# Low halves of ten FFN weight blocks by an accumulating DMA in a fused fp32 transformer step on one Trainium2 core

## The chip, the cores and the metric

The kernel runs on one core of a Trainium2 chip. The metric is the device time of one execution in microseconds (us); lower is better. Three executions of the kernel before took 1033.17, 1029.07 and 1034.92 us, median 1033.17.

## The reference, cut to what matters

One step of a small diffusion backbone: a mixing block (attention, S5 and RG-LRU scans) and then a convolutional gated FFN, over 640 tokens (128 context and 512 latent), all in fp32. The change touches the FFN only:

```python
def conv_ffn(h, lp):
    a, b = jnp.split(h @ lp['ffn_w_up'], 2, axis=-1)      # 640 x 1024 times 1024 x 5632
    a = dw_conv(a, lp['ffn_conv_w'], lp['ffn_conv_b'], 1, 1)
    return (jax.nn.gelu(a) * b) @ lp['ffn_w_down']        # 640 x 2816 times 2816 x 1024

h = rms_norm(x, lp['g2']) * (1 + sc2) + sh2
x = x + gt2 * conv_ffn(h, lp)
```

## The kernel before, in words

**Split products.** Every fp32 product is made of three TensorE products. A block is split into a high part, its rounding to the matmul type (`sh` for weights), and a low part, the block minus the high part (`sl`). The three products are high by high, high by low and low by high. `split` (L115) makes the two parts of a 128x512 weight block: the high part by an activation copy on ScalarE (ACT, helper line L79), the low part by a subtraction on VectorE (DVE, helper line L82). Both have six buffers.

**The FFN's up projection.** FF is 2816 = 22 tiles of 128 columns, numbered `fi`. For one tile the weights of both halves (a and b) are four 128x512 quarters `a11`, `a12`, `a21`, `a22` of two raw tiles `wr` (for the tiles 2 and 3 these are four tiles `wq`). Instead of eight quarter products the kernel makes seven, M1 to M7, in Winograd's way: sums of quarters (`sums_a`, `sums_b`, on VectorE and GpSimd) against sums of the four quadrants of the normalised tokens (`x_terms`). Each product M is 12 matmuls of 320 columns (`prod_mm`: for each of four k-slices high by high, high by low, low by high, in this order). M1, M2 and M3 use the quadrants as they are (`xbh`, `xbl`), M6, M7 and M5 use sums (`xth`, `xtl`).

**The stage of the change.** Between the output projection of the mixer and the steady run over the FFN tiles stands a hand-ordered head (L1619 to L1662), in which DVE, ACT and PE follow the program's order; POOL (GpSimd) does so in the whole kernel. The head takes the first two FFN tiles (fi 0 and 1, `NHEAD` is 2), while the normalisation of the last token tile (t = 4) is still under way. `prepare(n)` splits the next weight blocks, `early` issues their products, `post` adds them up. The order of blocks is M1 and M2 of tile 0, M1 and M2 of tile 1, then M3, M6, M7 of both:

```python
prepare(2)                      # split M1, M2 of tile 0
sums_b(0)                       # overwrites a11 and a12 of tile 0
out_mm(4, bl, 0, w_out2); norm2_t(3, ...); out_mm(4, bl, 1, w_out2)
out_res(4, bl, slice(512, 1024))
norm2(4, ...); prepare(4)       # split M1, M2 of tile 1
early(0, 1); sums_b(1); prepare(6)
norm2_t(4, None); early(2, 3)
early(4, 5); prepare(8); early(6, 7); prepare(10); early(8, 9)
```

The lines that only sum or split tokens are left out here. `sums_b(fi)` adds the sum `s2` to `a11` and subtracts it from `a12` in place; so it has to come after the splits of M1 and M2 have read these quarters, and M3 reads the `a12` that it leaves. `out_res(4)` makes the residual of the last token tile, `norm2(4)` its norm (a square sum on ACT, a power `rs` on POOL, a diagonal `dg` on DVE), and `norm2_t(4)` its transposes on PE and the scaling on ACT and DVE.

**DMAs.** The weights come by DMAs of the SP queue. POOL issues a few DMAs itself: eight accumulating ones `tsp<-tgate` (L541, SBUF to DRAM, 320 KB each) in the mixer and the loads `gt<-gdr` (L1147).

Of the kernel before, what the change touches and what calls it, by code (L numbers as in the profile page):

```python
# [18 lines left out]
MUL, ADD, SUB, MAX = ALU.mult, ALU.add, ALU.subtract, ALU.max  # L19
# [17 lines left out]
NPR = 3  # L37
S4F = 2
KPOW = 1
PREP_1 = 7  # L40
NB = 2
GE = True
# [5 lines left out]
NHEAD, LOOK, SA_AT, SB_AT = 2, 4, "M5", "M2"  # L48
# [23 lines left out]
def tile_hybrid_flow_step(ctx, tc, a, o):  # L72
    nc = tc.nc
    ctx.enter_context(tc.manual_schedule(engines={mybir.EngineType.Pool}))
    V, S, G, T, Q = nc.vector, nc.scalar, nc.gpsimd, nc.tensor, nc.sync
    SE, TE, FE, XE = V, V, V, G

    def act(out, in_, f=AF.Copy, **k):
        S.activation(out, in_, f, **k)  # L79

    def tt(out, x, y, op, e=V):
        e.tensor_tensor(out, x, y, op)  # L82
# [7 lines left out]
    def f(ap):  # L90
        return ap.bitcast(F32)
# [23 lines left out]
    def split(src, p=None, e=V):  # L115

        b, p = (6, pw) if p is None else (4, p)
        n = src.shape[-1]
        hi = p.tile([P, n], F32R, tag="sh", name="sh", bufs=b)
        act(hi, src)  # L120
        lo = p.tile([P, n], F32R, tag="sl", name="sl", bufs=b)
        tt(lo, src, f(hi), SUB, e)
        return hi, lo

    def wload(src, p=None):
        raw = raw_load(src)
        return [split(raw[:, z * 512:z * 512 + 512], p) for z in range(2)]
# [312 lines left out]
    def h_chunk(k, b, m2):  # L440
        b2 = b[:, 256:260]
        for q in range(2):
            mm(b2[:, 2 * q:2 * q + 2], m2[:, q * P:(q + 1) * P], sel[:, 0:2], True, True)
        sc = px.tile([P, 2], F32, tag="sc", name="sc", bufs=2)
        sh = px.tile([P, 2], F32, tag="sh", name="sh", bufs=2)
        ts(sh, b2[:, 0:2], pp("b_ada", k, 1), None, ADD, ALU.bypass)
        ts(sc, b2[:, 2:4], pp("b_ada", 8 + k, 1), 1.0, ADD, ADD)
        ts(sc, sc, pp("g1", k, 1), None, MUL, ALU.bypass)
        hf = px.tile([P, NT], F32, tag="hf", name="hf", bufs=2)
        for q, (n0, n1) in ((0, (NC_, NT)), (1, (0, NC_))):  # L450
            act(hh[:, k, n0:n1], xt[:, k, n0:n1], AF.Identity, scale=sc[:, q:q + 1], bias=sh[:, q:q + 1])
            ts(hf[:, n0:n1], xt[:, k, n0:n1], sc[:, q:q + 1], sh[:, q:q + 1], MUL, ADD)
        tt(hl[:, k], hf, f(hh[:, k]), SUB)
# [19 lines left out]
    for k in range(NK + 1):  # L473
        if k < NK:
            ads.append(ada_mm(k))
        if k < 2:
            h_chunk(k, *ads[k])
            if k == KPOW:
                s5_powers(px)
# [42 lines left out]
    def gate_half(br, c, h, x=None):  # L522

        if h == 0:
            state["wg"] = win(18 + 8 * br + c)
            state["tg"] = pv.tile([P, NT], F32, tag="tgate", name="tgate", bufs=2)
            if br:
                raw = pw.tile([P, 256], F32, tag="wr", name="wr", bufs=4)
                Q.dma_start(out=raw, in_=a["w_br"][c][:, 256 + 256 * br:512 + 256 * br])
                state["wb"] = split(raw)  # L530
        tg = state["tg"]
        n0, n1 = h * HT, (h + 1) * HT
        b = bank()
        dense_half(state["wg"], hh, hl, b[:, :HT], n0, n1)
        act(tg[:, n0:n1], b[:, :HT], AF.Tanh, scale=0.5)
        if br:
            b = bank()
            dense_half([state["wb"]], *x, b[:, :HT], n0, n1, nk=2)
            stt(tg[:, n0:n1], tg[:, n0:n1], 1.0, b[:, :HT], ADD, MUL)
        if h and br == 1:  # L540
            G.dma_start(out=tsp[16 + c], in_=tg, accum_op=ADD)  # L541
        elif h:
            Q.dma_start(out=tsp[8 * br + c], in_=tg)
# [118 lines left out]
    for i in range(2):  # L662
        b = dense_fm(win(12 + i), hh, hl)
        if i == 0:
            for _ in range(PREP_1):
                next(prep)
# [4 lines left out]
        for t0 in range(4):  # L671
            Q.dma_start(out=ut[32 * t0:32 * t0 + 32, 4 * i:4 * i + 4],
                        in_=udr[i].rearrange("(j f) t c -> t f j c", f=32)[t0])
    ylru = []

    def lru_tile(i):
# [9 lines left out]
        lw = pw.tile([P, 4, P], F32, tag="wr", name="lw", bufs=4)  # L686
        Q.dma_start(out=lw, in_=a["lru_w"][i])
        lwh, lwl = (x.rearrange("p (m c) -> p m c", m=4) for x in split(lw.rearrange("p m c -> p (m c)")))
        yield
        hs = []  # L690
# [596 lines left out]
    for qt in range(2):  # L1287
        w = [wload(a["w_out"][qt, kk]) for kk in range(2)]
# [31 lines left out]
    ups, s2s = {}, {}  # L1320
# [9 lines left out]
    def raw_free():  # L1330
        freed[0] += 1
        raw_pump()
# [11 lines left out]
    def quarters(fi):  # L1344
        if fi in AHEAD:
            return rawt["up", fi] + rawt["up", NF + fi]
        r0, r1 = rawt["up", fi], rawt["up", NF + fi]
        return r0[:, 0:512], r0[:, 512:], r1[:, 0:512], r1[:, 512:]

    def sums_a(fi):  # L1350

        a11, a12, a21, a22 = quarters(fi)
        tt(a21, a11, a21, SUB, SE)
        s2s[fi] = p1.tile([P, 512], F32, tag="s2", name="s2", bufs=2)
        tt(s2s[fi], a22, a21, SUB, SE)

    def sums_b(fi):

        a11, a12, a21, a22 = quarters(fi)
        s2 = s2s[fi]  # L1360
        tt(a11, s2, a11, ADD, SE)
        tt(a12, a12, s2, SUB, (V if fi < S4F else G))
# [5 lines left out]
    def prod_prep(fi, m):  # L1368
        a11, a12, a21, a22 = quarters(fi)
        if m == "M6" and fi not in s2s:  # L1370
            sums_a(fi)
        w = split({"M1": a11, "M2": a12, "M3": a12, "M4": a22, "M5": a11, "M6": s2s.get(fi), "M7": a21}[m])
        if fi >= NHEAD and m == SB_AT:
            sums_b(fi)
        if (m in ("M3", "M4") and fi >= NHEAD or m == "M4") and fi not in AHEAD:
            raw_free()
            if fi < NHEAD:
                raw_free()
        if m == SA_AT and NHEAD <= fi + 1 < NF and ("up", NF + fi + 1) in rawt:
            sums_a(fi + 1)  # L1380
        return w
# [123 lines left out]
    def add_up(fi, ms):  # L1505
        for m in ms:
            items.append((lambda fi=fi, m=m: prod_prep(fi, m), lambda w, fi=fi, m=m: prod_run(fi, m, w)))
# [278 lines left out]
```

## Time and profile before

| | before |
|---|---|
| three executions, us | 1033.17, 1029.07, 1034.92 |
| median, us | 1033.17 |
| the profiled execution's own time, us | 1037.32 |
| its span, us | 1035.6 |
| mean granted TensorE clock | 0.986 |
| PE busy | 996.1 us, 96% |
| VectorE (DVE) busy | 771.5 us, 74% |
| ScalarE (ACT) busy | 473.4 us, 46% |
| GpSimd (POOL) busy | 129.3 us, 12% |

The span is the time from the first to the last instruction of one profiled execution. Its own time of 1037.32 us is 4.15 us above the median of the three. The stage of the change lies between about 559 and 640 us of the span. PE's records there are read with care: matmuls are pipelined, so a busy PE need not be one at its peak, and idle time is what a wait shows.

### The profile page before, as it was taken

How to read it: one execution, taken by the hardware profiler on the slowest of the kernel's cores; microseconds unless marked ns; L12 is line 12 of the kernel's file. 1: busy time of each engine (PE TensorE's matmuls, PEld its weight loads, DVE VectorE, ACT ScalarE, POOL GpSimd, SP SyncE). 2: the span in 40 equal slices, each digit the busy share in tenths (PEclk: the TensorE clock that was granted, in tenths of full speed). 3: DMA queues.
4: the chain of work that ended last, by engine and by line, in shares of the span. 5: the costliest groups of instructions: out<-in, count | busy, mean ns of one | idle time of the engine just before them, and what ended most of it. 6: DMA issues, size and time to landing. Idle time of an engine off the chain costs nothing.

```text
span 1035.6 us, 17667 instructions
## 1 busy us (share of the span) xinstructions
PE 996.1 (96%) x6636; PEld 925.0 (89%) x6636; DVE 771.5 (74%) x1820; ACT 473.4 (46%) x919; POOL 129.3 (12%) x147
## 2 busy tenths in 40 slices
PE   5998999999999999999999989999999999999996
PEld 4788986879999999999899988988999899988995
DVE  6893787565846766657566599976998589966986
ACT  5253772224355555555332755532554145522543
POOL 6017500000002021101000201100110001100113
PEclk9998999999999999999999999999999999999998
DMA  9523357673245235434844131141324122331212
GB/s 363 217 82 88 97 169 247 228 238 115 77 131 170 76 100 136 117 81 115 291 142 142 51 129 47 41 143 34 92 82 123 58 69 79 99 102 48 95 63 102
DMA packets 50582, 126.31 MB, mean 122 GB/s; under 512 B 5536, under 2 KB 17728, under 8 KB 50496
## 3 DMA queue, kind: packets, MB, share of 16 engines
q1 hardware_dynamic: 48768, 120.46, 36.0%
q0 software_dynamic: 1728, 4.72, 2.2%
q8 instruction: 52, 0.85, 0.3%
q14 instruction: 34, 0.28, 0.1%
HBM read 111.10 MB, written 12.75 MB: 120 GB/s over the span
## 4 chain that ended last, share of the span: by engine, by line
PE 76%; DVE 10%; DMA 6%; ACT 3%; issue 2%; POOL 1%; SPq 1%; POOLq 0%; DVEq 0%; ACTq 0%
PE bk L94 34%; PE bM L94 23%; PE dn L94 14%; DMA wr<-in_w_in 3%; DVE sl L82 2%; DMA kc<-in_kct 1%; PE ptp L1066 1%; PE sc L94 1%; PE ob L94 1%; DMA xin<-in_x_sample 1%; PE gp L94 1%; ACT h L79 1%; DVE x L82 1%; ACT sh L79 1%; DVE tb L82 1%
## 5 line engine op out<-in xcount | busy, mean ns | idle before, releaser
L79 ACT ACTIVATE sh<-wr 128x512 fp32r<-128x512 f32 (+1 forms) x288 | 173.7, 616 | 226.9 <-PE dn L94 82.6
L82 DVE TENSOR_TENSOR sl<-wr,sh 128x512 fp32r<-128x512 f32 (+1 forms) x288 | 200.0, 704 | 81.5 <-ACT sh L79 80.9
L94 PE MATMUL bk<-hh,sl 128*128 128x320 f32 x608 | 189.7, 313 | 2.1 <-DVE sl L82 2.1
L94 PE MATMUL bk<-hh,sh 128*128 128x320 f32 x608 | 186.9, 316 | 3.1 <-ACT sh L79 3.0
L94 PE MATMUL bk<-hl,sh 128*128 128x320 f32 x608 | 189.3, 312 | 0.0
L94 PEld LDWEIGHTS bk<-hh,sh 128*128 128x128 f32 x608 | 114.0, 190 | 14.9 <-ACT sh L79 6.5
L94 PEld LDWEIGHTS bk<-hh,sl 128*128 128x128 f32 x608 | 115.4, 190 | 5.9 <-DVE sl L82 4.4
L94 PEld LDWEIGHTS bk<-hl,sh 128*128 128x128 f32 x608 | 115.6, 190 | 2.5 <-issue 0.8
L94 PE MATMUL bM<-xth,sl 128*128 128x320 f32 x352 | 109.2, 311 | 1.2 <-DVE sl L82 1.2
L94 PE MATMUL bM<-xtl,sh 128*128 128x320 f32 x352 | 108.9, 309 | 1.0 <-DVE xtl L82 1.0
L94 PE MATMUL bM<-xth,sh 128*128 128x320 f32 x352 | 108.9, 310 | 0.5 <-ACT sh L79 0.5
L94 PE MATMUL dn<-sh,ah 128*128 128x512 f32 (+1 forms) x224 | 87.1, 390 | 0.0
L94 PE MATMUL dn<-sl,ah 128*128 128x512 f32 (+1 forms) x224 | 87.1, 390 | 0.0
L94 PE MATMUL dn<-sh,al 128*128 128x512 f32 (+1 forms) x224 | 87.0, 389 | 0.0
L94 PE MATMUL bM<-xbh,sh 128*128 128x320 f32 x264 | 81.9, 310 | 1.3 <-ACT xbh L79 0.9
L94 PE MATMUL bM<-xbl,sh 128*128 128x320 f32 x264 | 81.6, 309 | 0.7 <-DVE xbl L82 0.7
L94 PE MATMUL bM<-xbh,sl 128*128 128x320 f32 x264 | 81.8, 310 | 0.4 <-DVE sl L82 0.3
L94 PEld LDWEIGHTS bM<-xth,sl 128*128 128x128 f32 x352 | 66.2, 188 | 2.3 <-DVE sl L82 2.2
L94 PEld LDWEIGHTS bM<-xtl,sh 128*128 128x128 f32 x352 | 66.2, 188 | 1.2 <-DVE xtl L82 1.2
L94 PEld LDWEIGHTS bM<-xth,sh 128*128 128x128 f32 x352 | 66.0, 188 | 1.3 <-ACT sh L79 1.0
L82 POOL TENSOR_TENSOR wr<-wr,s 128x512 f32<-128x512 f32 x18 | 27.4, 1524 | 315.6 <-DVE sl L82 269.2
L94 PEld LDWEIGHTS bM<-xbh,sh 128*128 128x128 f32 x264 | 49.6, 188 | 2.0 <-ACT xbh L79 1.2
(409 smaller groups left out, 2192.1 us busy)
## 6 DMA issues: line engine op xcount, KB each, us to landing
wr<-in_w_up SPq DMA_DIRECT2D x40, 512.0 KB
wr<-in_w_in SPq DMA_DIRECT2D x38, 512.0 KB
wr<-in_w_ada SPq DMA_DIRECT2D x32, 512.0 KB
wr<-in_w_down SPq DMA_DIRECT2D x22, 512.0 KB
adw<-in_w_ada SPq DMA_DIRECT2D x16, 512.0 KB
tsp<-tgate SPq DMA_DIRECT2D x16, 320.0 KB
wr<-in_w_out SPq DMA_DIRECT2D x8, 512.0 KB
tsp<-tgate POOLq DMA_DIRECT2D x8, 320.0 KB, 5.6
```

What stands on the lines that cost most here:

```text
L79: S.activation(out, in_, f, **k)
L82: e.tensor_tensor(out, x, y, op)
L94: T.matmul(out, l, r, start=start, stop=stop)
L1066: T.transpose(bt[:, c * P:(c + 1) * P], pr[:, c * P:(c + 1) * P], ident)
```

## The change

For ten blocks (M1, M2, M3, M6 and M7 of the FFN tiles 0 and 1) `split` is called with no engine. ACT then writes the negated high part into the low part's buffer (one more 128x512 activation), and POOL issues a DMA that adds the raw block onto it, SBUF to SBUF, 256 KB. M4 and M5 of these tiles and all other blocks keep the subtraction on VectorE.

```diff
--- before.py
+++ after.py
@@ -37,6 +37,7 @@
 NPR = 3
 S4F = 2
 KPOW = 1
+SPLIT_DMA = ("M1", "M2", "M3", "M6", "M7")
 PREP_1 = 7
 NB = 2
 GE = True
@@ -119,7 +120,11 @@
         hi = p.tile([P, n], F32R, tag="sh", name="sh", bufs=b)
         act(hi, src)
         lo = p.tile([P, n], F32R, tag="sl", name="sl", bufs=b)
-        tt(lo, src, f(hi), SUB, e)
+        if e is None:
+            act(lo, f(hi), scale=-1.0)
+            G.dma_start(out=f(lo), in_=src, accum_op=ADD)
+        else:
+            tt(lo, src, f(hi), SUB, e)
         return hi, lo
 
     def wload(src, p=None):
@@ -1369,7 +1374,8 @@
         a11, a12, a21, a22 = quarters(fi)
         if m == "M6" and fi not in s2s:
             sums_a(fi)
-        w = split({"M1": a11, "M2": a12, "M3": a12, "M4": a22, "M5": a11, "M6": s2s.get(fi), "M7": a21}[m])
+        w = split({"M1": a11, "M2": a12, "M3": a12, "M4": a22, "M5": a11, "M6": s2s.get(fi), "M7": a21}[m],
+                  e=None if fi < NHEAD and m in SPLIT_DMA else V)
         if fi >= NHEAD and m == SB_AT:
             sums_b(fi)
         if (m in ("M3", "M4") and fi >= NHEAD or m == "M4") and fi not in AHEAD:
```

**GpSimd (POOL)**, from the last token sums of t = 2 on (`h` is the tensor of normalised tokens, `rs` the norm of t = 4, `gt` the second gate). Before:

```order
L82 TENSOR_TENSOR h_6283<-h_6283 128x4x64 [waits DVE_49,Pool_49]
L82 TENSOR_TENSOR h_6283<-h_6283 128x4x64
L82 TENSOR_TENSOR rs<-v,nhalf 128x1 [waits DVE_49]
L1147 DMA gt_7002<-gdr 128x1024 [waits DMASW2_49,DMASW1_49,DMASW0_49]
L1147 DMA gt_7002<-gdr 128x1024 [waits DMASW3_49]
```

With the change:

```order
L83 TENSOR_TENSOR h_6283<-h_6283 128x4x64
L125 DMA sl<-wr 128x512 [waits DMAHW7_49,DMASW2_49,PE_49]
L125 DMA sl<-wr 128x512 [waits DMASW3_49,PE_49]
L83 TENSOR_TENSOR rs<-v,nhalf 128x1 [waits DVE_49]
L125 DMA sl<-wr 128x512 [waits DMASW4_49,DMAHW3_49,PE_49,Activation_49]
L125 DMA sl<-wr 128x512 [waits DMASW5_49,PE_49,Activation_49]
L125 DMA sl<-wr 128x512 [waits DMASW6_49,PE_49,Activation_49]
L125 DMA sl<-wr 128x512 [waits DVE_49,DMASW7_49,PE_49,Activation_49]
L125 DMA sl<-s_7012 128x512 [waits DMASW0_49,DMASW2_49,PE_49,Activation_49]
L125 DMA sl<-s_7015 128x512 [waits DMASW1_49,DMASW3_49,PE_49,Activation_49]
L125 DMA sl<-wr 128x512 [waits DMASW4_49,DMAHW2_49,PE_49,Activation_49]
L125 DMA sl<-wr 128x512 [waits DMASW5_49,DMAHW1_49,PE_49,Activation_49]
```

The ten DMAs stand in POOL's order behind the token sums of t = 2, two ahead of the norm of t = 4 and eight behind it; the gate's loads now follow all ten.

**VectorE (DVE)** behind the token splits of t = 2 (before: from the last of them on; `xbl` are such splits, `x` is the residual stream, `wr` and `s` the weight quarters and their sum). Before:

```order
L82 TENSOR_TENSOR xbl_6266<-h_6283,xbh_6263 128x4x64 [waits Activation_49]
L82 TENSOR_TENSOR x_6270<-bk,gt_6271 128x512 [waits PE_49]
L82 TENSOR_TENSOR x_6270<-x_6270,xin 128x512 [waits DMAHW5_49,DVE_49]
L82 TENSOR_TENSOR h_6283<-h_6283 128x4x128 [waits Activation_49]
L88 TENSOR_SCALAR v<-ss,ss_6284 128x1 [waits Activation_49]
L82 TENSOR_TENSOR h_6283<-h_6283 128x4x128 [waits DVE_49]
L88 TENSOR_SCALAR dg<-ident,rs 128x128 [waits Pool_49]
L82 TENSOR_TENSOR sl<-wr,sh 128x512 [waits Activation_49] x2
L82 TENSOR_TENSOR xbl_6266<-h_6283,xbh_6263 128x4x128 [waits Activation_49]
L82 TENSOR_TENSOR wr<-s_7015,wr 128x512 [waits DVE_49]
L82 TENSOR_TENSOR wr<-wr,s_7015 128x512 [waits DVE_49]
L82 TENSOR_TENSOR sl<-wr,sh 128x512 [waits Activation_49]
```

With the change:

```order
L83 TENSOR_TENSOR wr<-s_7012,wr 128x512 [waits DMASW2_49]
L83 TENSOR_TENSOR wr<-wr,s_7012 128x512 [waits DMASW3_49]
L83 TENSOR_TENSOR x_6270<-bk,gt_6271 128x512 [waits PE_49]
L83 TENSOR_TENSOR x_6270<-x_6270,xin 128x512 [waits DMAHW5_49,DVE_49]
L83 TENSOR_TENSOR h_6283<-h_6283 128x4x128 [waits Activation_49]
L89 TENSOR_SCALAR v<-ss,ss_6284 128x1 [waits Activation_49]
L83 TENSOR_TENSOR h_6283<-h_6283 128x4x128 [waits DVE_49]
L89 TENSOR_SCALAR dg<-ident,rs 128x128 [waits Pool_49]
L83 TENSOR_TENSOR xbl_6266<-h_6283,xbh_6263 128x4x128 [waits Activation_49]
L83 TENSOR_TENSOR wq<-wq 128x512 [waits DMAHW6_49,DMAHW0_49]
L83 TENSOR_TENSOR wr<-s_7015,wr 128x512 [waits DMASW4_49]
L83 TENSOR_TENSOR wr<-wr,s_7015 128x512 [waits DMASW5_49]
```

The subtractions are gone. The two sums of tile 0 (`wr<-s_7012`), which stood long before this place, now stand ahead of the residual of t = 4 and wait for DMAs of POOL (the waits DMASW2 and DMASW3); those of tile 1 wait for DMASW4 and DMASW5.

**ScalarE (ACT)** from the square sum of t = 4 on. Before:

```order
L79 ACTIVATE sq,ss<-x_6270 128x512 [waits DVE_49]
L79 ACTIVATE sh<-wr 128x512 [waits DMAHW3_49]
L79 ACTIVATE sh<-wr 128x512
L79 ACTIVATE xbh_6263<-h_6283 128x4x128 [waits Activation_49]
L79 ACTIVATE sh<-wr 128x512
L79 ACTIVATE sh<-wr 128x512 [waits DVE_49]
L79 ACTIVATE xth_7126<-h_6283 128x4x192 [waits PE_49,Pool_49]
L79 ACTIVATE h_6283<-bk,modt,a_6277 128x128 [waits PE_49]
```

With the change:

```order
L80 ACTIVATE sq,ss<-x_6270 128x512 [waits DVE_49]
L80 ACTIVATE sh<-wr 128x512 [waits DMAHW3_49]
L80 ACTIVATE sl<-sh 128x512 [waits Activation_49]
L80 ACTIVATE sh<-wr 128x512
L80 ACTIVATE sl<-sh 128x512 [waits Activation_49]
L80 ACTIVATE xbh_6263<-h_6283 128x4x128
L80 ACTIVATE sh<-wr 128x512
L80 ACTIVATE sl<-sh 128x512 [waits Activation_49]
L80 ACTIVATE sh<-wr 128x512 [waits DVE_49]
L80 ACTIVATE sl<-sh 128x512 [waits Activation_49]
L80 ACTIVATE xth_7130<-h_6283 128x4x192 [waits PE_49,Pool_49]
L80 ACTIVATE h_6283<-bk,modt,a_6277 128x128 [waits PE_49]
```

Each high part is followed by its negated copy `sl<-sh`; the high part that waits for DVE (M3 of tile 1, which reads a quarter that `sums_b(1)` writes) still stands ahead of the token work of t = 4.

## Rows read from the trace of the kernel before

**Rows 1.** The page: span, and busy time of two engines.

```profile
span 1035.6 us, 17667 instructions
...
PE 996.1 (96%) x6636; PEld 925.0 (89%) x6636; DVE 771.5 (74%) x1820; ACT 473.4 (46%) x919; POOL 129.3 (12%) x147
```

**Rows 2.** Windows: length, busy PE, PEld, DVE, ACT, POOL, clock, DMA share, GB/s.

```profile
592.00:616.00 24.00, 21.20 (x138) 19.44 (x136) 22.25 (x46) 16.57 (x32) 3.06 (x5) 1.00 0.29 92
616.00:640.00 24.00, 21.26 (x135) 19.86 (x136) 23.95 (x48) 11.99 (x19) 1.63 (x1) 1.00 0.31 107
640.00:660.00 20.00, 20.00 (x137) 19.87 (x136) 19.75 (x39) 9.94 (x17) 3.30 (x2) 1.00 0.01 1
```

**Rows 3.** Timeline of PE: start, length in us, then idle before and releaser.

```profile
592.02 0.31 PE L94 MATMUL bM<-xbh,sl 128*128 128x320 f32 x1
...
595.99 2.05 PE L94 MATMUL bk<-dg,x 128*128 128x128 f32 x16 [0.58 <-DVE dg L88]
...
602.45 0.41 PE L94 MATMUL bM<-xbh,sh 128*128 128x320 f32 x1 [0.90 <-ACT xbh L79]
603.55 0.41 PE L94 MATMUL bM<-xbl,sh 128*128 128x320 f32 x1 [0.69 <-DVE xbl L82]
603.80 0.31 PE L94 MATMUL bM<-xbh,sl 128*128 128x320 f32 x1
603.95 0.31 PE L94 MATMUL bM<-xbh,sh 128*128 128x320 f32 x1
...
616.67 0.41 PE L94 MATMUL bM<-xtl,sh 128*128 128x320 f32 x1 [0.97 <-DVE xtl L82]
```

**Rows 4.** Timeline of POOL: the last token sums of t = 2.

```profile
591.61 1.44 POOL L82 TENSOR_TENSOR h<-h 128x256 f32<-128x256 f32 x2 [0.76 <-DVE xbl L82]
```

**Rows 5.** The tile tsp on POOL: the accumulating DMAs, their issue, their landing.

```profile
L541 POOL DMA_DIRECT2D tsp<-tgate x8: 858/868/1078, 365.8 to 494.5; - x8
...
DMA to landing us min/median/max: 4.4/5.6/9.3
```

**Rows 6.** Timeline of DVE, 589 to 604 us.

```profile
591.93 0.69 DVE L82 TENSOR_TENSOR x<-bk,gt 128x512 f32<-128x512 f32 x1 [0.47 <-PE bk L94]
...
595.65 0.29 DVE L88 TENSOR_SCALAR dg<-ident,rs 128x128 f32<-128x128 f32 x1 [0.44 <-POOL rs L82]
...
598.26 0.68 DVE L82 TENSOR_TENSOR wr<-wr,s 128x512 f32<-128x512 f32 x1
...
599.46 0.68 DVE L82 TENSOR_TENSOR wq<-wq 128x512 f32<-128x512 f32 x1
...
602.81 0.68 DVE L82 TENSOR_TENSOR xbl<-h,xbh 128x512 fp32r<-128x512 f32 x1
```

**Rows 7.** Timeline of ACT, 593 to 609 us.

```profile
593.63 0.60 ACT L79 ACTIVATE sq<-x 128x512 f32<-128x512 f32 x1 [0.78 <-DVE x L82]
594.17 0.19 ACT L79 ACTIVATION_READ_ACCUMULATOR sq<-x 128x1 f32 x1
594.27 1.14 ACT L79 ACTIVATE sh<-wr 128x512 fp32r<-128x512 f32 x2
...
598.97 0.64 ACT L79 ACTIVATE sh<-wr 128x512 fp32r<-128x512 f32 x1 [2.54 <-DVE wr L82]
599.51 0.83 ACT L79 ACTIVATE xth<-h 128x768 fp32r<-128x768 f32 x1
...
606.67 1.14 ACT L79 ACTIVATE sh<-s 128x512 fp32r<-128x512 f32 x2
```

**Rows 8.** The tile sl on DVE, 591 to 616 us: ns min/median/max.

```profile
L82 DVE TENSOR_TENSOR sl<-wr,sh x8: 682/683/685, 595.8 to 614.4; 128x512 fp32r<-128x512 f32 x8
```

**Rows 9.** Windows of PE alone: length, busy, granted clock, DMA share, GB/s.

```profile
156.00:158.00 2.00, 0.39 (x6) 1.00 0.74 190
158.00:160.00 2.00, 2.00 (x12) 0.80 0.83 279
160.00:162.00 2.00, 2.00 (x6) 0.50 0.79 311
162.00:164.00 2.00, 2.00 (x14) 0.85 0.86 281
```

## The prediction

> **What bounds the kernel now.** I read the page first: of the span, PE is busy 96% and VectorE 74% [rows 1], so over the whole kernel TensorE is the bound. What the change is worth is read from its own stage, and the windows show it [rows 2]: from 592 to 616 us PE is busy 21.20 of 24 us, from 616 to 640 us 21.26 of 24, and from 640 us on 20.00 of 20. VectorE is busy 22.25, 23.95 and 19.75 us in the same windows. So VectorE is full there, but PE stands still for only 2.8 + 2.7 us. The timeline of PE shows whom it waits for [rows 3]: the diagonal `dg`, token splits of ACT and VectorE (`xbh`, `xbl`, `xtl`). Taking every wait in this stage away would give at most about 5.5 us. The reader is to see next that the removed subtractions run on an engine with little slack, while what replaces them has to pass two other engines and a transfer, in a stage where products start as soon as their blocks are ready.
>
> **What goes away.** Ten subtractions on VectorE. One lasts 683 ns [rows 8]; in a row they start 0.6 us apart, so some 6 us of VectorE. Two of them (M1, M2 of tile 0) ran long before the stage and were not waited for; I cost them at nothing. In 595.8 to 614.4 us stand eight `sl<-wr` [rows 8]; two of them are M5's and stay, and M6's two (`sl<-s`) go as well, so eight are taken out there. Their removal can only pay where PE waits for VectorE.
>
> **What comes.** Ten activations `sl<-sh` on ACT: two copies in a row take 1.14 us and the second starts 0.54 us after the first [rows 7], so 0.54 us each, 5.4 us in all; ACT is busy 16.57 of 24 us in that stretch [rows 2]. And ten DMAs on POOL. The trace has no SBUF-to-SBUF adding DMA. The nearest rows are the eight adding DMAs of 320 KB from SBUF to DRAM [rows 5]: POOL spends 0.86 us on an issue, and they land 4.4 to 9.3 us after it, median 5.6. From below: if all of the shortest time shrinks with the size (256 of 320 KB), 4.4 becomes 3.5. From above: 7.5, well over the median and short of the single worst. I take L = 5.0 us, between the median unscaled (5.6) and scaled (4.5), and keep 3.5 and 7.5 for the range.
>
> The Trainium skill, *DMA: Bandwidth & Descriptors* (section on the anatomy of one DMA, gpsimd path), prices such a DMA at about 2.0 us plus bytes over 436 GB/s. By that estimate 256 KB would land in 2.6 us and the sum below would be about +5 us instead of +14; for the 320 KB rows it gives 2.75 us, and the trace has 4.4 at best, so here the trace does not agree.
>
> **Where it stands in the order: three landings in a row.** I follow the new order of the three engines with the durations of before.
>
> *First wave (M1, M2 of tile 0).* ACT writes their negated parts well ahead of the stage, but POOL follows the program's order, and there the two DMAs stand behind the token sums of t = 2, which end at 591.61 + 1.44 = 593.05 us [rows 4]. With L they land at 598.05 and, one issue later, 598.9. PE reaches the first low part at 592.02 [rows 3] and now waits until 598.05: about 6 us, the largest new gap. It is done with both products at about 601.4 (22 of 24 matmuls at 0.15 us, the distance of two starts [rows 3]). On VectorE the two sums of tile 0 overwrite what these DMAs read, so they wait too, and the residual of t = 4 is queued behind them: it moves from 591.93 [rows 6] to 598.9 + 0.7 = 599.6, by 7.7 us. With it move the square sum on ACT (593.63 to 601.3) [rows 7], the norm on POOL (now behind two issues, which are over by then) and `dg` (595.65 to 603.3) [rows 6]. PE's transposes of t = 4 go from 595.99 to about 603.7 [rows 3].
>
> *Second wave (M1, M2 of tile 1; M3).* ACT's high part of M1 starts at 594.27 + 7.7 = 602.0 [rows 7]; with the negated copies the two low parts are ready for POOL at 603.05 and 604.1, and land at 608.05 and 609.1. VectorE's sums of tile 1 wait for them and end at 609.8; they ended at 598.26 + 0.68 = 598.94 [rows 6], so the shift has grown to 10.9. The sums of tile 2 that now stand ahead of them wait for loads that before were there by 599.46 [rows 6]; even 7.7 us later these are in time. ACT's high part of M3 of tile 1 waits for the sum, and everything of ACT behind it with it: 598.97 becomes 609.85, plus one copy, so the token split `xth` goes from 599.51 to 610.95 [rows 7], by 11.4. Behind it lie the scaling of t = 4, `xbh`, and VectorE's `xbl`, 602.81 to 614.25 [rows 6]. So PE's first M3 product goes on at 603.55 + 11.4 = 615.0 [rows 3] and the pair ends at about 618.5. The DMAs of M3 (the later one issued at 611.0, landed at 616.0) are hidden behind the first M3 product.
>
> *Third wave (M6, M7).* ACT's high part of M6 goes from 606.67 [rows 7] to 618.1; its negated copy is done at 619.2 and its DMA lands at 624.2; the following three, one high part and one copy (1.1 us) apart, at 625.3, 626.9 and about 628.3. PE has nothing from 618.8 until 624.2, then finishes M6 of tile 0 at 625.7 and the other three at 627.4, 629.2 and 631.0. M5, which went on at 616.67 [rows 3], now does so at 631.15: **14.5 us later**. VectorE is ready for M5 some 11 us later than before, so it isn't the one waited for. Each wave adds L, so the shift is about 3 L - 0.5 us.
>
> **What is given back.** PE arrives 14.5 us later, VectorE about 11, so VectorE has a lead of some 3.5 us in the stretch that was 616 to 640 us. Idle there was 24 - 21.26 = 2.74 us [rows 2], 0.67 of it before 616.67; the remaining **2.1 us** of waits for VectorE and ACT go. Behind 640 us PE was full [rows 2] and nothing more is won.
>
> **The clock.** After a stretch in which PE was busy 0.39 of 2 us, the granted clock was 0.80, 0.50 and 0.85 in the next three windows of 2 us, that is at the lower of its levels (1.2 of 2.4 GHz) for about 3.4 us, with PE busy [rows 9]. The new gaps of 6 and 5.4 us are longer. Where the clock is low behind the first two waves, PE's loss is covered by the wait for ACT and VectorE; behind the third it is not: 3.4 us at half speed lose **1.7 us** (0 if the low stretch falls into the gap, 3.4 if two such stretches follow).
>
> **The sum.** 14.5 - 2.1 + 1.7 = +14.1 us on the profiled execution's own 1037.3 us, so 1051.4. That execution is 4.15 us above the median of the three shown; against the median it is 1033.2 + 14.1 = **1047.3 us, about 1.4% slower**. Ends: L = 3.5 and no loss by the clock: 10.0 - 2.1 = +7.9, 1041. L = 7.5 and the full loss by the clock: 22.0 - 2.1 + 3.4 = +23.3, 1056.5.
>
> **The rivals.**
> *The transfers land early.* Against the rows 5, an SBUF-to-SBUF add might land in 2.6 us or less (this is also what the page cited above gives). Then 3 x 2.6 - 0.5 - 2.1 = +5.2 us, 1038.4, and shorter still it is within 0.5%. For it: no DRAM is written. Against it: all eight rows are over 4.4. Chance 0.09.
> *VectorE's relief is the larger term (not slower).* If the low parts were there before PE asked for them, all of PE's waits in 592 to 640 us that VectorE causes could go, at most the 5.5 us of rows 2: 1027.7. It decides at the first wave: the landing would have to come before 592.0, so the issue by 587.0 at L = 5.0, and POOL's order puts it at 593.05 at the earliest [rows 4]. With the DMAs on the path, L under 0.9 us would do for no loss (3 L - 0.5 below 2.1), about what POOL spends on the issue alone. Chance 0.04.
> *The transfers crawl.* Rows 5 have one of 9.3 us. If landings of 7.5 to 9.3 us are the rule (POOL's issues back to back, weight loads beside them), the shift is 22 to 27.4, less 2.1, plus the clock: 1055 to 1062. Chance 0.15.
>
> **How the numbers follow.** Forecast 0.72, early 0.09, relief 0.04, crawl 0.15. A measurement of this kernel can tell about 0.5%, 5.2 us, from no change. The forecast and the crawl are slower by more (0.87), as is a small part of the early case (0.01); the rest of the early case and part of the relief (0.02) are within it: 0.10; faster by more: 0.02. The range leaves out the relief, the lower part of the early case and the upper half of the crawl. It goes from 1038.5 (the early case at its upper end, and the lower end of the forecast less what the three executions scatter) to 1057.
>
> **What would show it.** In the changed profile: ten POOL DMAs `sl<-wr` landing about 5 us after issue; an idle PE of about 6 us from 592 on, released by such a DMA; the residual of t = 4 on VectorE about 7.7 us later, its sums released by DMAs; M5 going on at about 631; granted clock below 1 somewhere in 595 to 635; no waits of PE for VectorE in the steady stretch until M4 of tile 1. The prediction is wrong if the first DMA is issued well before 593, if landings are under 3 us, or if PE's gap is closed by other products.

## The result, and the profile after

The changed kernel takes **1046.26 us** (median of 4 runs, 1043.67 to 1052.16), beside 1032.55 us for the kernel before on the same chip: ratio **1.0129, 95% interval 1.0085 to 1.0173**. It is slower by some 13 us. The forecast was 1047.3 us.

The page of the changed kernel (profiled execution: 1045.33 us) answers to [rows 1]:

```profile
span 1043.6 us, 17698 instructions
...
PE 997.0 (96%) x6636; PEld 927.4 (89%) x6636; DVE 766.3 (73%) x1810; ACT 479.1 (46%) x929; POOL 140.1 (13%) x157
...
q0 software_dynamic: 3168, 7.34, 3.6%
```

and its list of DMA issues has two new rows (KB each, median us from issue to landing):

```profile
sl<-wr POOLq DMA_DIRECT2D x8, 256.0 KB, 4.4
sl<-s POOLq DMA_DIRECT2D x2, 256.0 KB, 3.5
```

VectorE has ten instructions and 5.2 us less than in [rows 1], ACT 5.7 us more, POOL ten instructions and 10.8 us more: the change does what it says. Where the time went is read in one stretch, from the start of POOL's norm of token tile 3 (`rs`, the last thing ahead of the change) to the start of ACT's copy of the first product of FFN tile 3 (`M<-bM`, behind all of it). I call it **the stretch** from here on. The windows of PE over it, first of the kernel before, then of the changed one (from:to, length, PE busy, granted clock, DMA share, GB/s):

```profile
586.75:641.60 54.85, 48.88 (x323) 1.00 0.28 92
```

```profile
580.45:649.91 69.46, 54.72 (x324) 0.88 0.44 110
```

The stretch is 14.61 us longer. PE stands still for 14.74 us of it (69.46 - 54.72) instead of 5.97, that is 8.77 us more; and the same products keep it busy 5.84 us longer, at a mean granted clock of 0.88 instead of 1.00. The execution before reached the stretch 6.30 us later (586.75 against 580.45), which is scatter between executions and not the change (run 7 below has the same code up to there as the changed kernel and reaches it at 588.37); so the spans differ by 8.0 us only, and to compare a time of after with one of before I add 6.30 to it.

PE's waits in the changed kernel, 586 to 660 us (total, times, longest, us):

```profile
PE bM L95 <- DMA sl<-wr: 7.8, 2, 4.2
PE bM L95 <- DMA sl<-s: 3.6, 1, 3.6
PE bM L95 <- DVE sl L83: 0.9, 2, 0.6
PE bk L95 <- DVE dg L89: 0.9, 1, 0.9
...
```

Three waits, 11.4 us together, end with an adding DMA. The timeline of PE shows their places, and what else it waits for (as in [rows 3]):

```profile
590.09 0.42 PE L95 MATMUL bM<-xbh,sl 128*128 128x320 f32 x1 [4.21 <-DMA sl<-wr]
...
596.00 2.05 PE L95 MATMUL bk<-dg,x 128*128 128x128 f32 x16 [0.88 <-DVE dg L89]
...
601.96 0.63 PE L95 MATMUL bM<-xbh,sl 128*128 128x320 f32 x1 [3.60 <-DMA sl<-wr]
...
608.87 0.41 PE L95 MATMUL bM<-xbl,sh 128*128 128x320 f32 x1 [0.41 <-DVE xbl L83]
...
617.15 0.64 PE L95 MATMUL bM<-xth,sl 128*128 128x320 f32 x1 [3.59 <-DMA sl<-s]
...
642.23 0.41 PE L95 MATMUL bM<-xth,sl 128*128 128x320 f32 x1 [0.58 <-DVE sl L83]
```

One wait for each wave: M1 of tile 0, M1 of tile 1, M6 of tile 0. The timeline of VectorE shows that it is held as well (against [rows 6]):

```profile
590.07 0.69 DVE L83 TENSOR_TENSOR wr<-s,wr 128x512 f32<-128x512 f32 x1 [4.91 <-DMA sl<-wr]
591.58 0.69 DVE L83 TENSOR_TENSOR wr<-wr,s 128x512 f32<-128x512 f32 x1 [0.82 <-DMA sl<-wr]
592.19 0.68 DVE L83 TENSOR_TENSOR x<-bk,gt 128x512 f32<-128x512 f32 x1
...
601.94 0.69 DVE L83 TENSOR_TENSOR wr<-s,wr 128x512 f32<-128x512 f32 x1 [3.37 <-DMA sl<-wr]
603.19 0.69 DVE L83 TENSOR_TENSOR wr<-wr,s 128x512 f32<-128x512 f32 x1 [0.56 <-DMA sl<-wr]
```

VectorE's sums overwrite blocks that the DMAs have still to read, so it waits 9.7 us in four places (the four rows with a wait; POOL's issue at 586.66 lies inside the first wait), and the residual of token tile 4 (592.19) stands behind the first two. Last, the tile `sl` on POOL, against [rows 5]:

```profile
L125 POOL DMA_DIRECT2D sl<-wr x8: 851/861/1176, 586.7 to 618.3; - x8
L125 POOL DMA_DIRECT2D sl<-s x2: 853/856/860, 613.8 to 615.0; - x2
...
DMA to landing us min/median/max: 3.2/4.0/6.1
```

### The profile page after: what moved, and what is told of

It is laid out like the page before. It is cut to its first block, busy times and chain, and to the rows that moved or that the text cites. A ratio compares the mean times of both kernels' runs of the same rounds, so it can differ in the third digit from the quotient of the medians.

```text
span 1043.6 us, 17698 instructions
## 1 busy us (share of the span) xinstructions
PE 997.0 (96%) x6636; PEld 927.4 (89%) x6636; DVE 766.3 (73%) x1810; ACT 479.1 (46%) x929; POOL 140.1 (13%) x157
## 4 chain that ended last, share of the span: by engine, by line
PE 76%; DVE 9%; DMA 7%; issue 3%; ACT 3%; SPq 1%; POOL 1%; POOLq 0%; DVEq 0%; ACTq 0%
PE bk L95 32%; PE bM L95 24%; PE dn L95 14%; DMA wr<-in_w_in 2%; DVE sl L83 1%; PE sc L95 1%; PE ptp L1071 1%; PE ob L95 1%; DMA xin<-in_x_sample 1%; DMA kc<-in_kct 1%; DVE x L83 1%; ACT h L80 1%; PE gp L95 1%; DMA gt<-gdr 1%; DVE tq L83 1%
## 5 line engine op out<-in xcount | busy, mean ns | idle before, releaser
L83 DVE TENSOR_TENSOR sl<-wr,sh 128x512 fp32r<-128x512 f32 (+1 forms) x280 | 194.3, 703 | 80.5 <-ACT sh L80 80.1
L95 PE MATMUL bM<-xbh,sl 128*128 128x320 f32 x264 | 84.0, 318 | 8.2 <-DMA sl<-wr 7.8
L95 PEld LDWEIGHTS bM<-xbh,sl 128*128 128x128 f32 x264 | 51.3, 194 | 9.1 <-DMA sl<-wr 8.3
```

The lines of the kernel that those rows point to most:

```text
L95: T.matmul(out, l, r, start=start, stop=stop)
```

## The experiments

Two measures are given for each: the time of all runs against the kernel before on the same chip, and the stretch in its profiled execution. The stretch is thus one execution each, without an interval. PE idle is the stretch less PE busy, the clock is the mean granted one. The last column is the ratio that the stretch alone would give (1 and its difference to 54.85 over 1033 us).

| Kernel | stretch us | PE busy | PE idle | clock | ratio of the times (95%) | by the stretch |
|---|---|---|---|---|---|---|
| before | 54.85 | 48.88 | 5.97 | 1.00 | 1 | 1 |
| the change | 69.46 | 54.72 | 14.74 | 0.88 | 1.0129 (1.0085 to 1.0173) | 1.0141 |
| 1 POOL's DMAs first | 63.50 | 53.81 | 9.69 | 0.89 | 1.0075 (1.0047 to 1.0103) | 1.0084 |
| 2 sums elsewhere, first try | 68.63 | 53.34 | 15.29 | 0.88 | 1.0116 (1.0084 to 1.0149) | 1.0133 |
| 3 M6, M7 only | 57.09 | 50.57 | 6.52 | 0.94 | 0.9991 (0.9964 to 1.0019) | 1.0022 |
| 4 copies, no DMA | 57.64 | 50.08 | 7.56 | 0.97 | 1.0018 (0.9993 to 1.0043) | 1.0027 |
| 5 M1, M2 only | 65.15 | 52.30 | 12.85 | 0.95 | 1.0100 (1.0065 to 1.0134) | 1.0100 |
| 6 M3 only | 55.48 | 48.86 | 6.62 | 1.00 | 1.0006 (0.9981 to 1.0030) | 1.0006 |
| 7 sums late | 63.17 | 52.16 | 11.01 | 0.89 | 1.0055 (1.0027 to 1.0082) | 1.0081 |
| 8 both | 59.41 | 50.36 | 9.05 | 0.94 | 1.0033 (1.0004 to 1.0061) | 1.0044 |
| 9 all early | 57.42 | 49.29 | 8.13 | 0.97 | 1.0034 (1.0012 to 1.0056) | 1.0025 |
| 10 third wave too | 58.09 | 49.92 | 8.17 | 0.97 | 1.0038 (1.0016 to 1.0061) | 1.0031 |

My theory is that the place of the transfers costs the time: each wave's landing holds PE, and the first two hold VectorE too. The rivals: that VectorE's hold lies beside PE's waits and costs nothing; that the added copies on ACT are the price; that the waves hide one another.

**1. POOL's first DMAs ahead of its token sums.**

```diff
             if t == 2:
-                x_terms(slice(n0, n1), XE)
+                state["xt2"] = slice(n0, n1)
...
         prepare(2)
+        x_terms(state.pop("xt2"), XE)
         sums_b(0)
```

> Edit: the first two adding DMAs stand ahead of the token sums of t = 2 in POOL's order; the ten DMAs themselves are kept. Measure beside the time: the head time, from POOL's norm of t = 3 (586.75 before, 580.45 with the change) to ACT's copy of M1 of tile 3 (641.60 and 649.91): 54.85 us before, 69.46 with the change. Theory (three landings in a row, each holding VectorE's or ACT's queue): the first pair is issued about 5.7 us earlier and lands about when PE asks for it; the residual of t = 4 moves forward by 5 to 6 us against the change, waves two and three stay. Head time 63 to 65 us, so about 5 us faster than the change, about 1041 us. Rival A (PE only waits for its own low parts, the hold on VectorE is nothing): only PE's first wait of 4.2 us goes, and since later waits remain the head time falls by at most 4.2, to 65.3 or more, with the residual of t = 4 unmoved. Rival B (the cost is ACT's ten copies and the clock, not the landings): no change, 69.

Measured: 63.50 us. POOL issues the first pair at 580.89, right behind the norm, and the 4.21 us wait is gone; the remaining waits for a DMA are 1.3 and 1.8 us. The residual of token tile 4 starts 7.10 us after the start of the stretch (587.43) where the change has 11.74, so it moved forward by 4.6 us, and rivals A (residual unmoved, 65.3 or more) and B (69) are out. So moving these two issues in POOL's order gives back 6 of the 14.6 us, part of it through VectorE. It isn't free: on PE's waits of this kernel, ACT and the diagonal now come first.

```profile
PE bM L95 <- ACT xbh L80: 2.6, 1, 2.6
PE bk L95 <- DVE dg L89: 2.1, 1, 2.1
PE bM L95 <- DMA sl<-s: 1.8, 1, 1.8
PE bM L95 <- DMA sl<-wr: 1.3, 1, 1.3
...
```

**2. Tile 0's sums out of place (first try).**

```diff
...
+        if fi == 0:
+            n11 = pp("cre", 0, 512)
+            n12 = p1.tile([P, 512], F32, name="nq")
+            tt(n11, s2, a11, ADD, SE)
+            tt(n12, a12, s2, SUB, V)
+            moved[fi] = (n11, n12)
+            return
```

> Edit: the two sums of tile 0 write to other storage instead of in place, so VectorE no longer waits for the first pair of adding DMAs; POOL's order and the ten DMAs are those of the change. Theory: PE still waits 4 us for the first low part, yet the residual of t = 4 is no longer held, the second wave starts 5 to 6 us earlier, and the head time falls from 69.46 to 62 to 65 us; about 1040 us. Rival A (PE's own waits are what counts, the hold on VectorE is nothing): head time stays 69. Rival B (ACT's copies and the clock): stays 69.

Measured: 68.63 us, a miss. The residual did come on time (585.60, and 6.34 later on the clock of before it is 591.94, as in [rows 6]). But VectorE then stood 8.34 us at a later load, in its timeline:

```profile
602.21 0.69 DVE L83 TENSOR_TENSOR wq<-wq 128x512 f32<-128x512 f32 x1 [8.34 <-DMA wq<-in_w_up]
```

and SyncE's queue shows why. Its waits in 560 to 640 us:

```profile
SPq L113 <- DMA sl<-wr: 31.1, 2, 18.6
```

With tile 0's raw buffer written no more, its next load moved ahead of six `wq` loads in SyncE's queue, and that load must wait until the adding DMAs have read the old block. The six loads, of which the first were issued at 573.28 in the changed kernel, all started behind it, at 592.04. One hold took the place of the other, so this run doesn't tell the theories apart; run 7 is its repair. It does show a third queue that waits until a DMA has read its source; in the changed kernel it waits so too, 9.0 us once.

**3. M6 and M7 only (the third wave).**

```diff
-SPLIT_DMA = ("M1", "M2", "M3", "M6", "M7")
+SPLIT_DMA = ('M6', 'M7')
```

> Edit: only M6 and M7 of the two tiles get their low part by an adding DMA (four of ten). Theory: one landing is left on the path (the third wave). PE waits some 3.4 us for the first M6 low part, of which 1.5 us are taken back where PE waited for M5's tokens before, and about 1 us more where PE waited for VectorE later: head time 55 to 58 us against 54.85, so 0 to 3 us slower than before, 1033 to 1036. Rival (each DMA costs alike, 14.6 us over ten): 54.85 + 5.8 = 60.7.

Measured: 57.09 us, with one wait of PE for a DMA of 2.69 us. The rival's 60.7 is out. The times show no difference (0.9991), less than the stretch gives; whether something outside the stretch gave it back, or this one execution is not typical, is not shown.

**4. ACT's copies without a DMA.** VectorE adds the block to the negated copy.

```diff
             act(lo, f(hi), scale=-1.0)
-            G.dma_start(out=f(lo), in_=src, accum_op=ADD)
+            tt(lo, src, f(lo), ADD, V)
```

> Edit: the ten blocks keep ACT's negated copy, but VectorE adds the raw block onto it in place of the DMA: ACT's cost without any DMA. Theory (the landings are the cost): ACT's ten copies are covered or cost up to 1.2 us where VectorE's subtraction waits for them: head time 55 to 57 us, time within 0.3% of before. Rival B (ACT's ten copies delay the token work, some 5.9 us of ACT on the path): head time 60 or more.

Measured: 57.64 us, between the bounds of both: the ten copies lengthen the stretch by 2.8 us without any DMA. PE waits 1.9 us for ACT's `xbh` instead of 0.9 [rows 3]. A part of the 2.8 us is peculiar to this run, since here VectorE waits for the copies as well, in its list of waits:

```profile
DVE sl L83 <- ACT sl L80: 1.1, 4, 0.5
```

**5. M1 and M2 only (the first two waves).**

```diff
-SPLIT_DMA = ("M1", "M2", "M3", "M6", "M7")
+SPLIT_DMA = ('M1', 'M2')
```

> Only M1 and M2 of the two tiles come by DMA: the first two waves. M3, M6 and M7 are subtracted on VectorE as before. My theory: the first two waves bring some 9.5 to 11 of the 14.6 us, the third some 3.5: stretch 64 to 66. Rival (the waits are not additive: TensorE would have waited for its inputs at M6 anyway): 68 to 70. Rival (the clock's low stretches behind the third landing matter most): under 63.

Measured: 65.15 us. Both rivals (68 to 70, under 63) are out. The parts nearly add up: 10.30 (this run) + 2.24 (run 3) + 0.63 (run 6) = 13.2 of 14.6 us.

**6. M3 only.**

```diff
-SPLIT_DMA = ("M1", "M2", "M3", "M6", "M7")
+SPLIT_DMA = ('M3',)
```

> Only M3 of the two tiles comes by DMA: two DMAs, whose landing lies beside the products of M1 and M2 in the order of TensorE's work, and whose source no later operation on VectorE writes before they land. My theory: an adding DMA costs nothing where TensorE has other work until it lands and nobody overwrites its source: stretch 54 to 56.5, time within 0.3 per cent of the kernel before. Rival (ScalarE's copies and POOL's issues cost by themselves at any place): 57 or more, time over 0.3 per cent longer. Rival (VectorE relieved of two subtractions on its critical stretch makes it faster): under 54.

Measured: 55.48 us and a ratio of 1.0006. The two DMAs land in 3.4 and 3.7 us and nobody waits for them. An adding DMA is nearly free where its landing and its source are in nobody's way; it brings nothing either.

**7. The sums out of the way, and late.**

```diff
+        if fi < NHEAD:
+            moved[fi] = pp("cre", 0, 512) if fi else p1.tile([P, 512], F32, name="nq")
+            tt(moved[fi], a12, s2, SUB, V)
+            return
...
         early(6, 7)
+        for fi in range(NHEAD):
+            a11 = quarters(fi)[0]
+            tt(a11, s2s[fi], a11, ADD, SE)
```

> Second try at taking VectorE's hold away alone. As in the change, all ten low parts come by an adding DMA, and SyncE's queue keeps the order it has in the change. But the sums that were written over a11 and a12 while adding DMAs still read them are out of the way: a12 - s2 of both tiles goes to a buffer of its own (free room for tile 0, a dead part of the parameter tile for tile 1), and a11 + s2, which only M5 needs, comes after the M6 and M7 copies. The stretch counted is the same as before (POOL norm of token tile 3 to ScalarE's copy of tile 3's first product: 54.85 in the kernel before, 69.46 in the change). My theory (the landings reach the path twice: TensorE's own wait for the low parts, and VectorE's wait for the source to be read, which delays the residual and norm of the last token tile and with it POOL's issue of the second wave): the residual of token tile 4 and its diagonal come on time, POOL issues the second wave some 6 us earlier, so that TensorE's second wait (3.6 us) shrinks to under 1.5, the first (4.2) and the third (some 3.5) stay: 61 to 64. Rival A (TensorE's three waits are the whole cost, VectorE's hold lies beside them): 67.5 to 70. Rival B (the moved sums cost as much as the hold, in VectorE's later work): residual on time, but the stretch still over 66, with VectorE or ScalarE as a new releaser of TensorE's waits.

Measured: 63.17 us. PE's waits in this kernel:

```profile
PE bM L95 <- DMA sl<-wr: 5.4, 1, 5.4
PE bM L95 <- DMA sl<-s: 3.6, 1, 3.6
PE bM L95 <- DVE sl L83: 0.9, 2, 0.6
...
```

The second wave's wait is gone, as is any wait of VectorE for an adding DMA, with every DMA kept. The residual starts 5.18 us after the start of the stretch (593.55), just as before the change, and POOL issues the second wave 6.4 us earlier in the stretch than the change does (597.40). So VectorE's hold was worth some 6.3 us, through the residual, the norm and the place of the second wave in POOL's queue. This falsifies the rival that it lay beside PE's waits. Two things blur the number. The first wait was expected to stay at 4.2 us and is 5.4, since the first DMA now lands in 4.6 us. And two additions of 0.68 us have moved to a later place, which could explain at most 1.4 us; the kernel before with these moves was not run.

**8. Runs 1 and 7 together.** The two diffs of above.

> The edit of the run before, and POOL's eight operations of token tile 2 put behind the issue of the first two DMAs, so that the first wave is issued some 5 us earlier as well. My theory: with the first landing over before TensorE comes to it and VectorE not held, only the third wave (M6 and M7, 2 to 3.5 us) is left, with ScalarE's added copies (2.8 us in the run that had the copies without DMAs): 57 to 60. Rival A: the two edits touch the same 6 us, so that the second adds nothing to the first: 62 to 64. Rival B: ScalarE's copies and POOL's later operations take the place of the waits: 60 to 62 with those named as releasers of TensorE's waits.

Measured: 59.41 us, as the theory had it, but by other steps: the first wave no longer holds PE, while the second does again, in PE's timeline:

```profile
602.62 0.42 PE L95 MATMUL bM<-xbh,sl 128*128 128x320 f32 x1 [4.03 <-DMA sl<-wr]
```

PE now comes to tile 1 earlier, while POOL still issues its DMAs behind the norm of token tile 4, at 596.07.

**9. The second wave ahead of that norm** (the edit against run 8).

```diff
         x_terms(state.pop("xt2"), XE)
+        prepare(4)
```

> The version with POOL's first two DMAs ahead and the sums out of the way kept one long wait of TensorE, 4.03 us for tile 1's low parts, though VectorE was not held: POOL issues them behind the norm of the last token tile, and they landed in 6.5 us beside weight loads. Here ScalarE's copies of tile 1's M1 and M2 come before the norm of the last token tile instead of behind it, so that POOL issues their DMAs ahead of that norm, some 2.5 us earlier. My theory (what is left of the cost is the place of the issue): that wait shrinks to under 1.5 us, the norm comes 1 to 1.6 us later behind the copies, and the stretch falls from 59.41 to 56.5 to 58. Rival (the copies before the norm cost what the wait gives back): 58.8 or more, with the diagonal of the last token tile as releaser of a wait over 2 us.

Measured: 57.42 us; of the DMAs only the third wave (3.59 us) still holds PE. The rival's sign came as well, a wait of 2.05 us for the diagonal, but not its price (58.8 or more). The times don't follow run 8's stretch down (1.0034 after 1.0033), but the intervals are wider than 2 us.

**10. The third wave early as well** (the edit against run 9).

```diff
         early(2, 3)
+        prepare(8)
         post(0, 2)
...
         early(4, 5)
-        prepare(8)
```

> As the run before, and ScalarE's copies for M6 of both tiles come right behind TensorE's M1 and M2 of tile 1 instead of behind M3, so that POOL issues the DMAs of the third wave some 4 us earlier. Then all ten landings should be over when TensorE comes to them. My theory: the stretch falls by another 1.5 to 3 us to 54.5 to 56.5, at the kernel before's 54.85 within 1.7, and the time is within 0.3 per cent of the kernel before: all of the change's cost is where its transfers stand, none is left, and the two fifths of a microsecond per subtraction that VectorE saves buy nothing. Rival A (ScalarE's added copies keep a price that no place takes away, 2.8 us as in the run with copies and no DMAs): 57 to 59. Rival B (VectorE's saved time shows once nothing waits for a transfer): under 54 and over 0.3 per cent faster than the kernel before.

Measured: 58.09 us, my theory's miss. No wait of PE for a DMA is left, and the kernel is still 0.38% slower than before. PE's waits:

```profile
PE bM L95 <- ACT xth L80: 2.3, 1, 2.3
PE bk L95 <- DVE dg L89: 2.1, 1, 2.1
PE bM L95 <- DVE xtl L83: 1.3, 2, 1.0
...
```

The stretch lies where rival A has it (57 to 59): some 3 us stay, as in run 4. That they are the price of the copies wherever they stand is not shown. What now delays the token splits `xth` is ACT's row of operations for M6 of both tiles, 602.19 to 604.56, and half of it are the high parts, which the kernel before has as well, at a later place. The early place and the copies are not told apart; the kernel before in this order was not run. No version with DMAs beat the kernel before, so none is offered.

## Why the prediction was right

The direction and the mechanism held, and the size with some luck (at the end of the list): three landings in a row, with the norm's chain on VectorE behind the first. Step by step (times of after with 6.30 added):

- **First wave.** Predicted: issued at 593.05, landed at 598.05. Measured 592.96, and the landing took 3.4 us instead of 5.0, so PE waited 4.21 us, not 6. The residual came at 598.5 (predicted 599.6), the diagonal at 602.0 (603.3). PE's wait for it was 0.88 us where 2.3 was counted, since PE ran the first wave at the low clock; that loss was covered, as predicted.
- **Second wave.** Issued at 602.1 (predicted 603.05), but beside weight loads it landed in 6.1 us, so at 608.2 (608.05). VectorE's sums ended at 610.2 (609.8), and the M3 product went on at 615.2 (615.0), released by `xbl` as predicted.
- **Third wave.** The DMA was issued 0.9 us later than counted (620.1 against 619.2; the high part starts 0.5 us later, and it, its copy and the hand-over to POOL take 1.6 us, not 1.1) and landed in 3.3 us, so PE went on at 623.45 (predicted 624.2).
- **L.** The three landings on the path took 3.4, 6.1 and 3.3 us: 12.8 in sum for an assumed 15.0. One number for all was wrong in each case, by -1.6, +1.1 and -1.7 us, and the errors cancelled in part.
- **The clock.** 1.7 us was counted behind the third landing. After the wait of 3.59 us the windows of PE show the lower of its two levels (0.50, 1.2 of 2.4 GHz) until some 621.6 (from:to, length, PE busy, clock, DMA share, GB/s):

```profile
616.00:618.00 2.00, 0.85 (x3) 0.50 1.03 174
618.00:620.00 2.00, 2.00 (x10) 0.50 0.88 146
620.00:622.00 2.00, 2.00 (x10) 0.59 1.07 132
622.00:624.00 2.00, 2.00 (x16) 1.00 0.97 288
```

  Two matmuls then start 0.27 us apart instead of 0.15, and from the landing to M5 PE takes 9.0 us instead of the 6.95 counted without the clock: 2.1 us. The losses behind the first two waves, which bring PE's additional busy time to 5.84 us, were covered by VectorE's lateness; the step stands.
- **Given back.** 2.1 us were counted. At M5 the shift was 15.8 us and over the stretch 14.6: 1.2 us. Three waits of 1.24 us in all for VectorE's `sl` and ACT's `sh` stayed, the first at 642.23. The step "VectorE has a lead of some 3.5 us" took all of them for waits that a lead removes; why these stay was not tried.

So the terms 14.5 - 2.1 + 1.7 = 14.1 came out as 13.7 - 1.2 + 2.1 = 14.6 (13.7 is the measured shift at M5 less the clock). The sum was near because its errors have both signs, which is luck.

What the prediction lacked: the copies on ACT as a cost of their own. It counted them inside the waves; runs 4 and 10 show that 2.8 to 3.2 us stay when no transfer is waited for, though neither has the copies as its only difference (see there).

**The rivals.** *Early landing* (2.6 us or less) did not occur: 3.2 us is the shortest landing of an adding DMA in any of the kernels. *VectorE's relief*: 5.2 us of VectorE's time went away and bought nothing that was seen, in runs 6, 9 and 10 either. *Crawl*: not in the change (6.1 at most), but in run 2 a landing took 9.6 us.

## What to carry to other kernels

A subtraction of 0.68 us that is handed to a DMA becomes a copy, an issue in another engine's queue, and a landing of 3 to 6 us; that can pay only where the consumer comes later than the landing. M3's two were of that kind (run 6, in which only they come by DMA), and they brought nothing either. Ask in the profile for each such transfer what stands ahead of its issue in that queue, who writes its source next, and which queues (loads too) wait for that write: POOL's order and VectorE's hold were worth about 6 us each here, 10 together. Put a price on what feeds the transfer as well, since the kernel was still slower when all waits for the transfers were gone (run 10), and with the copies alone it had a stretch 2.8 us longer (run 4).

## What the runs showed of the hardware

- **An adding DMA moves its bytes at about half the rate of a load.** In the third wave of the changed kernel, with only adding DMAs in flight, a window (columns as in [rows 2]) shows the DMA engines full at 170 GB/s. In run 3 a window with only the weight loads `wq<-in_w_up` shows 305 GB/s, and in run 6 one with only POOL's loads of the gate, `gt<-gdr`, 350:

```profile
617.00:619.00 2.00, 1.85 (x7) 1.85 (x8) 2.00 (x4) 1.51 (x3) 1.30 (x3) 0.50 1.00 170
```

```profile
591.00:593.00 2.00, 1.44 (x13) 1.26 (x12) 1.60 (x4) 1.19 (x3) 0.36 (x1) 1.00 1.00 305
```

```profile
604.00:606.00 2.00, 2.00 (x15) 2.00 (x15) 1.93 (x3) 0.00 (x0) 0.00 (x0) 1.00 0.97 350
```

  The Trainium skill, *Collectives: The Full Stack* (Part 3, the bandwidth ceiling), says of a reduction that its add needs two source reads where a copy needs one, and that this halves the rate. Against the loads the rows agree with it (170 of 305 and of 350). But the loads come from DRAM and the adds from SBUF. The nearest plain copy from SBUF to SBUF is `qh<-qh` in the attention (SP queue, 160 KB, 64 partitions to 64), alone in a window of the kernel before:

```profile
391.40:393.40 2.00, 2.00 (x16) 2.00 (x15) 1.12 (x4) 0.72 (x4) 0.00 (x0) 1.00 0.65 145
```

  At a full share that would be an estimate of 223 GB/s (145 over 0.65), so that the adds have some three quarters of the rate of this copy, not half. The two differ in size, partitions and queue too; what the add alone costs is not shown.
- **Its landing went with what flowed beside it.** In the changed kernel and in runs 1 to 3 and 7 to 9 the first three DMAs of the third wave, with no load beside them, landed in 3.3 to 3.4, 3.7 and 3.6 us; the fourth, behind these and right ahead of the gate's loads, in 4.6 to 4.7. Beside the `wq` loads the DMAs of M1 and M2 of tile 1 took 6.1 us in the changed kernel (share 0.87 to 1.14 there) and 5.1 to 6.6 us in runs 1, 5, 7 and 8; in run 2, beside six loads, one took 9.6. That the loads are the cause was not tried alone. The Trainium skill, *DMA: Bandwidth & Descriptors* (anatomy of one DMA), would give 2.6 us for 256 KB, by a fixed part of 2.0 us and 436 GB/s; the trace doesn't agree for an add. With the bytes counted twice the estimate is 3.2 us, which is the shortest landing measured; that this is the reason is not shown.
- **Whoever writes the source next waits for the landing.** VectorE stood 9.7 us for it in the changed kernel, and SyncE's queue 18.6 us in run 2. The wait can begin before the issue: of the 18.6 us, which end at 591.65, 13.6 lie ahead of POOL's issue at 586.63.
